# A two-layer encoder on one core: the last MLP's second product by Strassen's scheme, in chunks interleaved with the first product

## The chip, the cores and the metric

One Trainium2 chip, of which the kernel uses one core. The metric is the device time in microseconds of one execution of the whole program; the time before is the median of three runs.

## The reference

An encoder of two layers on 512 tokens of width 1024, in float32. Layer 0 mixes tokens by a retention and a sliding-window attention, layer 1 by an axial attention; each layer ends with an MLP of width 4096 with a squared ReLU. What matters here is the second line of the MLP:

```python
D_MODEL = 1024; SEQ = 512; DEPTH = 2; D_FF = 4 * D_MODEL

for layer in range(DEPTH):
    h = rms_norm(x, norm_mix[layer])
    ...
    x = x + y
    h = rms_norm(x, norm_mlp[layer])
    x = x + jnp.square(jax.nn.relu(h @ w_mlp_up[layer])) @ w_mlp_down[layer]
return x
```

Per layer `w_mlp_up` is 1024x4096 and `w_mlp_down` 4096x1024.

## The kernel before, in words

**Products.** TensorE multiplies in a rounded float32 form (fp32r). To keep float32's accuracy every operand is split into a high part, its rounded copy, and a low part, the rest; a product of two operands is three matmuls into one bank, high x high, high x low, low x high (`mm3`, L309). The high parts are written by casts on ScalarE, the low parts by subtractions on VectorE. A bank is a PSUM tile of 128x512; there are eight.

**Weights.** `w_stream` (L383) brings the weights in units of 256 rows by 512 columns, 512 KB: SyncE's queue loads a unit into one of two `raw` tiles, ScalarE casts it (`wh`, L406), VectorE subtracts (`wl`, L408). There are four pairs of `wh` and `wl` (the w pairs), given in turn to the units in the order of a list, `plan`; this cast and subtraction are called the unit's cut below. `gemm` (L413) makes a 512x512 result in four banks, in steps of 512 along the contracted dimension, two units a step.

**The MLP.** `mlp` (L1157) goes over D_FF in two halves. In each half four up products (h times W_up, 96 matmuls each) make 2048 rows of the hidden layer. Their results leave the banks by a ReLU and scaling on VectorE (L1168), a square on ScalarE (L1171) and a split into one of four `big` pairs (L299, L304). Then two down products of 192 matmuls (512 columns of the result each) run over the 2048. In the last MLP `last` (L1320) adds each bank to the accumulator `acc_o` (L1325), and in the second half stores the result (L1329). The very last 128 rows of the last down product are made in two halves of 256 columns (`halves=True`): 96 of that MLP's matmuls have 256 columns.

**What sets the order.** The kernel's parts are generators, run at build time by `Weave` (L120), a planner: each step says which engine it needs and for how long, by the costs of `vec`, `act` and `pe` (L189 to L198), and the planner always writes the instruction that can start first on its own clock. What it wrote is each engine's fixed order on the chip. Casts and subtractions of W carry a bias that lets other work go ahead unless the unit is among the next to be used. Products of the attention stages are woven in the same way with gemms that make the projections.

Of the kernel before, what the change touches and what calls it, by code (L numbers as in the profile page):

```python
# [12 lines left out]
F32 = mybir.dt.float32  # L13
F32R = mybir.dt.float32r
AF = mybir.ActivationFunctionType
# [48 lines left out]
class Slots:  # L64


    def __init__(self, weave, items):
        self.weave, self.waiting = weave, []
        self.free = [(0.0, i) for i in range(len(items))]
        self.items = items  # L70
        self.index = {id(x): i for i, x in enumerate(items)}

    def ask(self, task):
        if not self.free:
# [111 lines left out]
            self.advance(task, op[0])  # L186


def vec(n, scalars=0, rate=0.96):  # L189
    return ("V", 0.065 + n / rate / 1000 + 0.065 * scalars)  # L190


def act(n, extras=0):
    return ("A", 0.075 + n / 1200 + 0.093 * extras)


def pe(n):
    return ("P", 3 * (n / 2400 + 0.0025))  # L198


TRANSPOSE = 0.11
# [13 lines left out]
def hybrid_encoder(ctx: ExitStack, tc: tile.TileContext, a, out):  # L215
# [13 lines left out]
    psp = ctx.enter_context(tc.tile_pool(name="psp", bufs=1, space=PS))  # L229

    W = Weave()

    def slots(name, n, shape, dt, pool=cst):
# [11 lines left out]
    probs_t = pairs("pt", 3, (P, 512))  # L245
    temps = slots("t", 11, (P, 512), F32)
    gates = slots("g", 4, (P, 512), F32)
    hs = [(cst.tile([P, 512], F32R, name=f"hh{k}"), cst.tile([P, 512], F32R, name=f"hl{k}")) for k in range(KD)]
    xT = [cst.tile([P, 512], F32, name=f"xT{k}") for k in range(KD)]
    rB = cst.tile([P, 512], F32, name="rB")  # L250

    def kv_pair():
# [56 lines left out]
    def mm3(o, l, r, first, last):  # L309
        (lh, ll), (rh, rl) = l, r  # L310
        nc.tensor.matmul(o, lhsT=lh, rhs=rh, start=first, stop=False)  # L311
        nc.tensor.matmul(o, lhsT=lh, rhs=rl, start=False, stop=False)  # L312
        nc.tensor.matmul(o, lhsT=ll, rhs=rh, start=False, stop=last)  # L313

    def transposed(bank, parts):
        for j, p_ in enumerate(parts):
# [61 lines left out]
    w_used = [0]  # L378
    def landed(ev):
        yield Sleep(W.now + LANDING)  # L380
        ev.set()

    def w_stream():  # L383

        arrived = [W.event() for _ in plan]
        raw_of = [None] * len(plan)

        def loads():
            yield opened
            for i in range(2, len(plan)):  # L390
                raw_of[i] = yield raws
                yield Sleep(W.now + 1.2)
                yield ("D", 1.5)
                nc.sync.dma_start(out=raw_of[i], in_=plan[i][1].rearrange("(k p) n -> p k n", p=P))
                W.spawn(landed(arrived[i]), LOAD)
                if i == 3:
                    w_begun.set()

        W.spawn(loads(), LOAD)
        for i in range(2, len(plan)):  # L400
            pair = yield wparts
            yield arrived[i]
            hi, lo = pair
            hold = lambda: LOAD_BIAS if i >= w_used[0] + 2 else -1.0
            yield act(1024) + (hold,)
            nc.scalar.copy(out=hi, in_=raw_of[i])  # L406
            yield vec(1024) + (hold,)
            nc.vector.tensor_tensor(out=lo, in0=raw_of[i], in1=hi.bitcast(F32), op=ALU.subtract)  # L408
            raws.give(raw_of[i])
            w_tiles[i] = pair  # L410
            w_ready[i].set()

    def gemm(name, r0, r1, c0, lhs, natural, evac, cls=EVAC, bk=None, halves=False):  # L413

# [739 lines left out]
        bigs.give(y)  # L1154


    def mlp(l, h_ev, rB_ev, last, after=None):  # L1157
        for hf in range(2):
            u, u_ready = [], []
# [177 lines left out]
    def products():  # L1337
# [66 lines left out]
        W.spawn(natural_xs(hn_ready), AUX)  # L1404
# [62 lines left out]
```

## Time and profile before

| | |
|---|---|
| median of three runs | 1261.37 us (1261.25 to 1261.75) |
| the profiled execution | 1261.47 us, its span 1259.7 us |
| TensorE matmuls (PE) | 1254.3 us busy, 5880 instructions |
| TensorE weight loads (PEld, beside matmuls) | 1043.9 us busy |
| VectorE (DVE) | 698.7 us busy, 55% |
| ScalarE (ACT) | 526.8 us busy, 42% |
| GpSimd (POOL) | 1.6 us busy |
| granted TensorE clock | 1.00 on the mean |

The span is what the profiler saw of the kernel, from the first to the last instruction; the device time of the same execution is 1.8 us longer. Matmuls are pipelined: one of 512 columns is listed with some 0.39 us, while the next starts 0.23 us behind it, so what one costs is read from the distance of two starts. In the rows further down, "PE" are matmuls, "PEld" weight loads, and L-numbers are lines of the kernel. The number ahead of an operation in the timeline is its start from the begin of the span, the next its length; brackets tell what it waited for, where the profile shows one.

### The profile page before, as it was taken

What the parts mean: (1) busy time and instruction counts of PE and PEld (TensorE: products, weight loads), DVE (VectorE), ACT (ScalarE), POOL (GpSimd) and SP (SyncE); (2) the same over time, 40 slices, a digit from 0 to 9 for tenths busy, and PEclk for the clock granted to TensorE, in tenths of its full rate; (3) what the DMA queues carried; (4) which work ended last, traced back from release to release, by engine and by line L of the source; (5) the groups of instructions that cost most, each with busy time, mean ns of one, the idle gap of its engine ahead of it and who ended that gap; (6) DMA issues with size and microseconds to landing.
All of it is one profiled execution on the core that took longest, in us unless ns stands there. A gap on an engine that the chain in (4) does not pass through costs nothing.

```text
span 1259.7 us, 15049 instructions
## 1 busy us (share of the span) xinstructions
PE 1254.3 (100%) x5880; PEld 1043.9 (83%) x5880; DVE 698.7 (55%) x1248; ACT 526.8 (42%) x1015; POOL 1.6 (0%) x10
## 2 busy tenths in 40 slices
PE   9999999999999999999999999999999999999998
PEld 7888888888888888888888888888888888888887
DVE  6698668767676452324444268897745422444331
ACT  6676424344344342224333245776544311244210
POOL 0000000000000000000000000000000000000000
PEclk9999999999999999999999999999999999999999
DMA  6521322222143333233333233111323233333331
GB/s 187 182 87 35 101 84 84 67 84 84 50 126 96 90 96 101 89 98 100 101 100 101 85 89 95 34 34 34 101 84 85 100 100 100 100 100 99 101 120 51
DMA packets 63896, 115.13 MB, mean 91 GB/s; under 512 B 5245, under 2 KB 11431, under 8 KB 63568
## 3 DMA queue, kind: packets, MB, share of 16 engines
q1 hardware_dynamic: 63824, 114.16, 29.3%
q8 instruction: 46, 0.75, 0.2%
q14 instruction: 26, 0.21, 0.1%
HBM read 112.03 MB, written 4.21 MB: 92 GB/s over the span
## 4 chain that ended last, share of the span: by engine, by line
PE 99%; DMA 0%; ACT 0%; SPq 0%; issue 0%; DVE 0%
PE bank L311 31%; PE bank L313 31%; PE bank L312 31%; PE bank L317 4%; PE bank L534 1%; DMA x_nat<-in_x_dram 0%; SPq L493 0%; PE bank L1114 0%; ACT pth L299 0%; PE bank L654 0%; PE bank L1141 0%; ACT t L1271 0%; DVE acc_o L1325 0%; PE bank L605 0%
## 5 line engine op out<-in xcount | busy, mean ns | idle before, releaser
L408 DVE TENSOR_TENSOR wl<-raw,wh 128x1024 fp32r<-128x1024 f32 x198 | 240.7, 1219 | 302.0 <-ACT wh L406 299.6
L406 ACT CAST wh<-raw 128x1024 fp32r<-128x1024 f32 x198 | 207.6, 1051 | 385.0 <-PE bank L312 228.1
L311 PE MATMUL bank<-hh,wh 128*128 128x512 f32 x512 | 200.7, 392 | 0.0
L313 PE MATMUL bank<-hh,wl 128*128 128x512 f32 x512 | 199.3, 389 | 0.0
L312 PE MATMUL bank<-hl,wh 128*128 128x512 f32 x512 | 199.2, 389 | 0.0
L311 PE MATMUL bank<-bigh,wh 128*128 128x512 f32 x448 | 176.0, 393 | 0.0
L313 PE MATMUL bank<-bigh,wl 128*128 128x512 f32 x448 | 174.6, 390 | 0.0
L312 PE MATMUL bank<-bigl,wh 128*128 128x512 f32 x448 | 174.4, 389 | 0.0
L311 PE MATMUL bank<-wh,hh 128*128 128x512 f32 x368 | 146.5, 398 | 0.0
L313 PE MATMUL bank<-wh,hl 128*128 128x512 f32 x368 | 143.8, 391 | 0.0
L312 PE MATMUL bank<-wl,hh 128*128 128x512 f32 x368 | 143.5, 390 | 0.0
L311 PEld LDWEIGHTS bank<-hh,wh 128*128 128x128 f32 x512 | 96.1, 188 | 20.1 <-issue 0.5
L313 PEld LDWEIGHTS bank<-hh,wl 128*128 128x128 f32 x512 | 96.1, 188 | 20.1
L312 PEld LDWEIGHTS bank<-hl,wh 128*128 128x128 f32 x512 | 96.1, 188 | 20.0 <-issue 0.5
L312 PE MATMUL bank<-wl,bigh 128*128 128x512 f32 (+1 forms) x272 | 102.5, 377 | 0.0
L311 PE MATMUL bank<-wh,bigh 128*128 128x512 f32 (+1 forms) x272 | 102.4, 377 | 0.0
L313 PE MATMUL bank<-wh,bigl 128*128 128x512 f32 (+1 forms) x272 | 102.4, 377 | 0.0
L313 PEld LDWEIGHTS bank<-bigh,wl 128*128 128x128 f32 x448 | 84.1, 188 | 17.7
L311 PEld LDWEIGHTS bank<-bigh,wh 128*128 128x128 f32 x448 | 84.1, 188 | 17.0 <-DVE ptl L304 0.3
L312 PEld LDWEIGHTS bank<-bigl,wh 128*128 128x128 f32 x448 | 84.2, 188 | 16.9
L313 PEld LDWEIGHTS bank<-wh,hl 128*128 128x128 f32 x368 | 69.1, 188 | 14.8
L311 PEld LDWEIGHTS bank<-wh,hh 128*128 128x128 f32 x368 | 69.1, 188 | 14.3 <-issue 0.9
(175 smaller groups left out, 1569.9 us busy)
## 6 DMA issues: line engine op xcount, KB each, us to landing
raw<-in_w_mlp_up_dram SPq DMA_DIRECT2D x64, 512.0 KB, 3.7
raw<-in_w_mlp_down_dram SPq DMA_DIRECT2D x64, 512.0 KB, 4.4
raw<-in_w_in_even_dram SPq DMA_DIRECT2D x35, 512.0 KB, 4.0
raw<-in_w_out_even_dram SPq DMA_DIRECT2D x16, 512.0 KB, 3.6
raw<-in_w_in_odd_dram SPq DMA_DIRECT2D x12, 512.0 KB, 3.7
raw<-in_w_out_odd_dram SPq DMA_DIRECT2D x8, 512.0 KB, 3.5
bdr<-bdr SPq DMA_DIRECT2D x2, 1024.0 KB, 6.1
out_dram<-acc_o SPq DMA_DIRECT2D x7, 256.0 KB, 2.0
```

Source lines behind the costliest of these rows:

```text
L311: nc.tensor.matmul(o, lhsT=lh, rhs=rh, start=first, stop=False)
L312: nc.tensor.matmul(o, lhsT=lh, rhs=rl, start=False, stop=False)
L313: nc.tensor.matmul(o, lhsT=ll, rhs=rh, start=False, stop=last)
L317: nc.tensor.transpose(bank[:, j * P:(j + 1) * P], p_, ident)
L406: nc.scalar.copy(out=hi, in_=raw_of[i])
L408: nc.vector.tensor_tensor(out=lo, in0=raw_of[i], in1=hi.bitcast(F32), op=ALU.subtract)
L534: nc.tensor.matmul(first_bk[b], lhsT=hs[k][i == 2][:, b * P:(b + 1) * P], rhs=wt, start=k == 0 and i == 0, stop=False)
```

## The change

The second product of the last MLP is done by Strassen's scheme in Winograd's form: 2x2 blocks, seven products in place of eight, with sums of blocks ahead and behind. D_FF is taken in four chunks of 1024. In a chunk, the left operand's blocks are halves of the tokens (256) and of the chunk (512); the right operand's are halves of the chunk and of the columns (512). A product is 24 matmuls of 512 columns: two W units (h = 0, 1), for each two blocks of 128 tokens, two of 128 rows, three matmuls. Partial sums of the results stay in the banks: product 6 goes on in the banks of product 1 after these have been read, 7 in those of 6, 3 in those of 5.

- **Order of the products.** up(0), then for each chunk q: up(2q+1), products 2, 1, 4, then up(2q+2) if q < 3, then products 6, 5, 7, 3. The last chunk has no up product between products 4 and 6.
- **Sums of the hidden layer** (A, B, C, D): 64 operations of 128x256 on VectorE (`minus`, line 1325 of the changed kernel), and the splits that follow them.
- **Sums of W.** Two of the four block sums, used by products 7 and 5, are made by negating a loaded unit in place on ScalarE and adding another from DRAM with an accumulating DMA (`added`) of 512 KB, issued from GpSimd's queue: 16 of them. The other two, used by products 6 and 4, are made by VectorE (16 operations of 128x1024). So W_down is cut into 56 units in place of 32.
- **Adds of the results**: 64 of 128x512 (`add`, line 1398), in place of 15 of 128x512 and 2 of 128x256.
- **Room.** `g` and the probabilities of the attention get tiles of a size that the last MLP can use as five more raw tiles; the tiles of x^T serve as raw tiles and for a sum, too.
- **The planner.** `pe(512)` goes from 0.6475 to 0.6805 us for three matmuls in the whole program; the fixed part of `vec` and `act` goes to 0.15 and 0.19 us in the last MLP alone. Since the price of a matmul is new everywhere, the planner's order changes in all stages.

```diff
+FIXED = [0.065, 0.075]
+
+
 def vec(n, scalars=0, rate=0.96):
-    return ("V", 0.065 + n / rate / 1000 + 0.065 * scalars)
+    return ("V", FIXED[0] + n / rate / 1000 + 0.065 * scalars)
 
 
 def act(n, extras=0):
-    return ("A", 0.075 + n / 1200 + 0.093 * extras)
+    return ("A", FIXED[1] + n / 1200 + 0.093 * extras)
 
 
 def pe(n):
-    return ("P", 3 * (n / 2400 + 0.0025))
+    return ("P", 3 * (n / 2400 + 0.0135))
...
+    def shared(i, dt):
+        return cst.tile([P, 2, 512], dt, tag=f"sh{i}", name=f"sh{i}")
+
+    gs = [shared(i, F32) for i in range(2)]
+    pts = [shared(i, F32R) for i in range(2, 5)]
+    probs_t = Slots(W, [(t[:, 0, :], t[:, 1, :]) for t in pts])
...
+    gates = Slots(W, [t[:, j, :] for t in gs for j in range(2)])
...
-    plan += plan_mlp(1)
...
+    PRODUCTS = (2, 1, 4, 6, 5, 7, 3)
...
+    plan_up(0)
+    for q in range(4):
+        plan_up(2 * q + 1, [(q, r, c, h) for r, c in ((0, 1), (0, 0), (1, 0)) for h in range(2)])
+        plan_products(q, PRODUCTS[:3])
+        last_two = [(q, 1, 1, h) for h in range(2)]
+        if q < 3:
+            plan_up(2 * q + 2)
+        for at in last_two:
+            chunk_at[at] = len(loads_of)
+            loads_of.append(quarter(*at))
+        plan_products(q, PRODUCTS[3:])
...
+        def added(out, q, r, c, h):
+
+            yield ("D", 1.6)
+            nc.gpsimd.dma_start(out=out, in_=quarter(q, r, c, h).rearrange("(k p) n -> p k n", p=P), accum_op=ALU.add)
+            yield Sleep(W.now + 4.5)
...
+        def t1(q, h, st):
+
+            x = raw_of[chunk_at[q, 0, 0, h]]
+            yield st["cut", 1]
+            yield st["t2"]
+            yield act(1024) + due(q, 5, h, 6)
+            nc.scalar.mul(x, x, -1.0)
+            yield from added(x, q, 0, 1, h)
+            st["src", 5].set()
+
+        def sums(q, h, st):
+
+            r11, r12, r21, r22 = (chunk_at[q, r, c, h] for r in range(2) for c in range(2))
+            yield arrived[r12]
+            t3 = raw_of[r12]
+            yield act(1024)
+            nc.scalar.mul(t3, t3, -1.0)
+            yield from added(t3, q, 1, 1, h)
+            st["src", 7].set()
+            yield arrived[r11]
+            st["src", 1].set()
+            W.spawn(t1(q, h, st), LOAD)
+            t2 = st["x"] = yield xs
+            yield vec(1024) + due(q, 4, h, 6)
+            nc.vector.tensor_tensor(out=t2, in0=t3, in1=raw_of[r11], op=ALU.add)
+            st["src", 6].set()
+            st["t2"].set()
+            yield st["cut", 2]
+            t4 = raw_of[r21]
+            yield vec(1024) + due(q, 4, h, 4)
+            nc.vector.tensor_tensor(out=t4, in0=t4, in1=t2, op=ALU.subtract)
+            st["src", 4].set()
+            yield st["cut", 4]
+            raws.give(t4)
+            yield st["cut", 6]
+            xs.give(t2)
+            for pr, n in ((5, r11), (7, r12), (3, r22)):
+                yield st["cut", pr]
+                raws.give(raw_of[n])
...
+        def cut(i, pair, ready, get, done):
+            yield ready
+            hi, lo = pair
+            src = get()
+            hold = lambda: LOAD_BIAS if i >= w_used[0] + 2 else -1.0
+            yield act(1024) + (hold,)
+            nc.scalar.copy(out=hi, in_=src)
+            yield vec(1024) + (hold,)
+            nc.vector.tensor_tensor(out=lo, in0=src, in1=hi.bitcast(F32), op=ALU.subtract)
+            done()
+            w_tiles[i] = pair
+            w_ready[i].set()
...
+            def minus(out, x, y, op=ALU.subtract):
+                yield vec(256)
+                nc.vector.tensor_tensor(out=out, in0=x, in1=y, op=op)
...
+            def rest(i, t_, f):
+                c = yield temps
+                yield ev["A", i]
+                yield from minus(c[:, half[0]], t_[:, half[1]], f[:, half[1]], ALU.add)
+                yield from minus(c[:, half[1]], c[:, half[0]], t_[:, half[0]])
+                yield from split(*part("C", i, slice(0, 512)), c, 512)
+                ev["1", i].set()
+                W.spawn(rest2(i, t_, f, c), AUX)
+
+            def rest2(i, t_, f, c):
+                yield from minus(t_[:, half[0]], t_[:, half[0]], t_[:, half[1]])
+                yield from minus(f[:, half[0]], f[:, half[0]], c[:, half[1]])
+                temps.give(c)
+                yield from split(*part("A", i, half[1]), t_[:, half[0]], 256)
+                temps.give(t_)
+                ev["3", i].set()
+                yield from split(*part("D", i, half[0]), f[:, half[0]], 256)
+                ev["D", i].set()
+                temps.give(f)
...
+            of = {1: ("A", "A", 0, "X", True, ((0, 0),)), 2: ("B", "B", 0, "Y", True, ((0, 0),)),
+                  4: ("B", "B", 1, "V", True, ((1, 0),)), 6: ("C", "1", 1, "X", False, ((0, 1),)),
+                  5: ("C", "1", 0, "Z", True, ((1, 1),)), 7: ("A", "3", 1, "X", False, ((1, 0), (1, 1))),
+                  3: ("D", "D", 0, "Z", False, ((0, 1),))}
+            open_, read = {}, {}
...
+            def add(tb, bank, outs, closes, stores):
+                for rc_ in outs:
+                    t, c = 2 * rc_[0] + tb, rc_[1]
+                    o = acc_o[t, c]
+                    yield acc_ready[t, c]
+                    yield vec(512)
+                    nc.vector.tensor_tensor(out=o, in0=bank, in1=o, op=ALU.add)
+                    if closes and rc_ == outs[-1]:
+                        gbanks.give(bank)
+                    if stores:
+                        yield ("D", 0.8)
+                        nc.sync.dma_start(out=out[0, t * P:(t + 1) * P, c * 512:(c + 1) * 512], in_=o)
...
+            for pr in PRODUCTS:
+                name, evn, hf, bn, opens, rc_ = of[pr]
+                ws = []
+                for h in range(2):
+                    n = w_used[0] + h
+                    assert plan[n][0] == ("down1", q, pr, h), (plan[n][0], q, pr, h)
+                    yield w_ready[n]
+                    ws.append(w_tiles[n])
+                    for tb in range(2):
+                        if h == 0:
+                            if opens:
+                                open_[bn, tb] = yield gbanks
+                            else:
+                                yield read[bn, tb]
+                        for ii in range(2):
+                            i = 2 * h + ii
+                            yield ev[evn, i]
+                            uh, ul = ub[name]
+                            us = slice(hf * 256 + tb * P, hf * 256 + (tb + 1) * P)
+                            yield pe(512)
+                            mm3(open_[bn, tb], (uh[:, i, us], ul[:, i, us]), (ws[h][0][:, ii, :], ws[h][1][:, ii, :]),
+                                opens and i == 0, i == NT - 1, skip_group_check=not opens)
+                        if h == 1:
+                            read[bn, tb] = W.spawn(add(tb, open_[bn, tb], rc_, pr in (2, 4, 7, 3), q == 3 and pr in (1, 3, 7)), EVAC)
+                    wparts.give(ws[h])
+                w_used[0] += 2
+                for n in {7: "A", 5: "C", 3: "D", 4: "B"}.get(pr, ""):
+                    bigs.give(ub[n])
+                if pr == 4 and q < 3:
+                    yield from up(2 * q + 2, lambda i, bank, st=state[q + 1]: up1(i, bank, st))
...
-        yield from mlp(1, hn_ready, rB1, last)
+        yield from last_mlp(hn_ready, rB1)
```

**The last chunk on VectorE.** First the end of VectorE's order before: cuts of W, and the adds of the last down product.

```order
L408 TENSOR_TENSOR wl_80<-raw_77,wh_79 128x1024
L408 TENSOR_TENSOR wl_82<-raw_78,wh_81 128x1024
L408 TENSOR_TENSOR wl_84<-raw_77,wh_83 128x1024
L408 TENSOR_TENSOR wl_86<-raw_78,wh_85 128x1024
L1325 TENSOR_TENSOR acc_o<-bank_74,acc_o 128x512
L1325 TENSOR_TENSOR acc_o<-bank_69,acc_o 128x512
L1325 TENSOR_TENSOR acc_o<-bank_70,acc_o 128x512
L1325 TENSOR_TENSOR acc_o<-bank_71,acc_o 128x256
L1325 TENSOR_TENSOR acc_o<-bank_72,acc_o 128x256
```

Then VectorE's order in the changed kernel, from the second cut of product 5 (wl_86) on, in the last chunk: wl_80 is the low half of product 7's first unit, whose pair product 6's first unit held; bigl_90 is the low half of C, bigl_92 and bigl_94 are those of A and D; line 538 is the subtraction of a cut, 319 that of a split.

```order
L538 TENSOR_TENSOR wl_86<-xs_6823,wh_85 128x1024
L1325 TENSOR_TENSOR t_102<-t_102 128x256
L1325 TENSOR_TENSOR t_103<-t_103 128x256
L1325 TENSOR_TENSOR t_107<-t_107,t_109 128x256
L538 TENSOR_TENSOR wl_80<-sh_6526,wh_79 128x1024
L1325 TENSOR_TENSOR t_109<-t_110,t_105 128x256
L319 TENSOR_TENSOR bigl_92<-t_102,bigh_91 128x256
L1325 TENSOR_TENSOR t_109<-t_109,t_110 128x256
L1325 TENSOR_TENSOR t_106<-t_106,t_101 128x256
L319 TENSOR_TENSOR bigl_94<-t_107,bigh_93 128x256
L1325 TENSOR_TENSOR t_100<-t_100 128x256
L319 TENSOR_TENSOR bigl_90<-t_109,bigh_89 128x512
```

Where VectorE had cuts and adds alone, the cut of a later product now stands ahead of the sums and the split of the last quarter of C.

**The first axial group on TensorE.** ident transposes a block of q into a bank, which is then cast and subtracted into bigh_87 and bigl_88; kv and bigh_87 make the scores of a head; wh and hh are a projection. Before:

```order
L317 MATMUL bank_72<-ident,t_104 128x128 x4
L311 MATMUL bank_70<-wh_81,hh_120 128x512
L312 MATMUL bank_70<-wl_82,hh_120 128x512
L313 MATMUL bank_70<-wh_81,hl_121 128x512
L311 MATMUL bank_70<-wh_81,hh_122 128x512
L312 MATMUL bank_70<-wl_82,hh_122 128x512
L313 MATMUL bank_70<-wh_81,hl_123 128x512
L311 MATMUL bank_69<-kv,bigh_87 128x512
L312 MATMUL bank_69<-kv,bigh_87 128x512
L313 MATMUL bank_69<-kv,bigl_88 128x512
L311 MATMUL bank_72<-kv,bigh_87 128x512
```

The same place in the changed kernel:

```order
L332 MATMUL bank_75<-ident,t_100 128x128 x4
L326 MATMUL bank_69<-kv,bigh_87 128x512
L327 MATMUL bank_69<-kv,bigh_87 128x512
L328 MATMUL bank_69<-kv,bigl_88 128x512
L326 MATMUL bank_75<-kv,bigh_87 128x512
```

The bank of the transposes is used for scores nine matmuls later before, and three matmuls later now.

## Rows read from the trace of the kernel before

**Rows 1.** The page, part 1: busy time, share of the span, instructions.

```profile
PE 1254.3 (100%) x5880; PEld 1043.9 (83%) x5880; DVE 698.7 (55%) x1248; ACT 526.8 (42%) x1015; POOL 1.6 (0%) x10
```

**Rows 2.** The page, part 4: the chain that ended last, by engine.

```profile
PE 99%; DMA 0%; ACT 0%; SPq 0%; issue 0%; DVE 0%
```

**Rows 3.** Table of stretches (us): length, busy time and instructions by engine.

```profile
core 0: us, PE busy (x) PEld busy (x) DVE busy (x) ACT busy (x) POOL busy (x), PEclk, DMA share, GB/s
925.00:1200.00 275.00, 275.00 (x1215) 227.72 (x1214) 107.02 (x120) 89.75 (x112) 0.00 (x0) 1.00 0.31 96
760.00:880.00 120.00, 119.92 (x605) 98.58 (x604) 103.30 (x264) 83.36 (x220) 0.00 (x0) 1.00 0.14 45
60.00:150.00 90.00, 90.00 (x477) 77.16 (x476) 75.47 (x249) 59.07 (x173) 0.00 (x0) 1.00 0.25 74
1256.00:1258.00 2.00, 0.51 (x5) 0.31 (x3) 0.42 (x1) 0.00 (x0) 0.00 (x0) 1.00 0.26 91
1258.00:1259.70 1.70, 0.00 (x0) 0.00 (x0) 0.00 (x0) 0.00 (x0) 0.00 (x0) 0.85 0.16 52
...
770.00:790.00 20.00, 20.00 (x96) 15.99 (x95) 19.32 (x65) 15.23 (x55) 0.00 (x0) 1.00 0.22 73
```

**Rows 4.** Waits of TensorE's weight loads, 30 to 1250 us: total, times, longest.

```profile
PEld bank L311 <- ACT t L1271: 1.1, 3, 0.5
PEld bank L311 <- DVE ptl L304: 0.5, 2, 0.3
```

**Rows 5.** Timeline of TensorE, around the first matmul of 256 columns.

```profile
1241.51 0.39 PE L313 MATMUL bank<-wh,bigl 128*128 128x512 f32 x1
1241.74 0.39 PE L311 MATMUL bank<-wh,bigh 128*128 128x512 f32 x1
...
1242.53 0.28 PE L312 MATMUL bank<-wl,bigh 128*128 128x256 f32 x1
1242.65 0.28 PE L313 MATMUL bank<-wh,bigl 128*128 128x256 f32 x1
```

**Rows 6.** Groups by line and shape: count, busy us, mean ns, idle before.

```profile
L304 DVE TENSOR_TENSOR bigl<-t,bigh 128x512 fp32r<-128x512 f32 x64 | 44.3, 692 | 49.4 <-ACT bigh L299 49.4
...
L299 ACT CAST bigh<-t 128x512 fp32r<-128x512 f32 x64 | 39.8, 622 | 2.0
...
L1325 DVE TENSOR_TENSOR acc_o<-bank,acc_o 128x512 f32<-128x512 f32 x15 | 10.4, 692 | 35.3 <-PE bank L313 35.3
...
L1325 DVE TENSOR_TENSOR acc_o<-bank,acc_o 128x256 f32<-128x256 f32 x2 | 0.8, 424 | 1.8 <-PE bank L313 1.8
```

**Rows 7.** Timeline of ScalarE and VectorE in the last MLP: one W unit's cut.

```profile
938.75 1.05 ACT L406 CAST wh<-raw 128x1024 fp32r<-128x1024 f32 x1 [6.33 <-PE bank L312]
939.84 1.22 DVE L408 TENSOR_TENSOR wl<-raw,wh 128x1024 fp32r<-128x1024 f32 x1 [6.16 <-ACT wh L406]
```

**Rows 8.** DMA issues: count, KB of each, median us from issue to landing.

```profile
raw<-in_w_mlp_down_dram SPq DMA_DIRECT2D x64, 512.0 KB, 4.4
...
bdr<-bdr SPq DMA_DIRECT2D x2, 1024.0 KB, 6.1
out_dram<-acc_o SPq DMA_DIRECT2D x7, 256.0 KB, 2.0
x_nat<-in_x_dram SPq DMA_DIRECT2D x3, 512.0 KB, 8.7
...
out_dram<-acc_o SPq DMA_DIRECT2D x2, 128.0 KB, 1.7
```

**Rows 9.** Timeline in the first axial group: transposes, cast, subtract, scores.

```profile
781.81 0.60 PE L317 MATMUL bank<-ident,t 128*128 128x128 f32 x4
...
782.45 0.58 ACT L299 CAST bigh<-bank 128x512 fp32r<-128x512 f32 x1 [0.66 <-PE bank L317]
...
783.07 0.69 DVE L304 TENSOR_TENSOR bigl<-bank,bigh 128x512 fp32r<-128x512 f32 x1
...
784.34 0.39 PE L311 MATMUL bank<-kv,bigh 128*128 128x512 f32 x1
```

**Rows 10.** Timeline at the end: the last matmul and the last add.

```profile
1256.23 0.28 PE L313 MATMUL bank<-wh,bigl 128*128 128x256 f32 x1
1256.55 0.42 DVE L1325 TENSOR_TENSOR acc_o<-bank,acc_o 128x256 f32<-128x256 f32 x1 [1.01 <-PE bank L313]
```

More of the change, by code (lines that the diff above doesn't have):

```diff
@@ L71, in __init__, with add @@
         self.index = {id(x): i for i, x in enumerate(items)}
+    def add(self, item):
+        self.index[id(item)] = len(self.items)
+        self.items.append(item)
+        self.give(item)
     def ask(self, task):
@@ L307, in split, with mm3 @@
                                            op0=ALU.mult, op1=ALU.subtract)
-    def mm3(o, l, r, first, last):
+    def mm3(o, l, r, first, last, **kw):
         (lh, ll), (rh, rl) = l, r
-        nc.tensor.matmul(o, lhsT=lh, rhs=rh, start=first, stop=False)
-        nc.tensor.matmul(o, lhsT=lh, rhs=rl, start=False, stop=False)
-        nc.tensor.matmul(o, lhsT=ll, rhs=rh, start=False, stop=last)
+        nc.tensor.matmul(o, lhsT=lh, rhs=rh, start=first, stop=False, **kw)
+        nc.tensor.matmul(o, lhsT=lh, rhs=rl, start=False, stop=False, **kw)
+        nc.tensor.matmul(o, lhsT=ll, rhs=rh, start=False, stop=last, **kw)
     def transposed(bank, parts):
@@ L373, in hybrid_encoder, with plan_w, quarter, plan_up @@
             plan += w_parts("w_out_odd", r0, r0 + 512, c0)
-    plan += plan_mlp(1)
+    PRODUCTS = (2, 1, 4, 6, 5, 7, 3)
+    chunk_at = {}
+    loads_of = [ap for _, ap in plan]
+    def plan_w(parts):
+        plan.extend(parts)
+        loads_of.extend(ap for _, ap in parts)
+    unit_load = list(range(len(plan)))
+    at_product = {}
+    def quarter(q, r, c, h):
+        r0 = q * 1024 + (1 - r) * 512 + h * 256
+        return a["down1"][r0:r0 + 256, c * 512:c * 512 + 512]
+    def plan_up(g, between=()):
+        between = list(between)
+        for part in w_parts("up1", 0, D, g * 512):
+            for at in between[:1]:
+                chunk_at[at] = len(loads_of)
+                loads_of.append(quarter(*at))
+            del between[:1]
+            unit_load.append(len(loads_of))
+            plan_w([part])
+        for at in between:
+            chunk_at[at] = len(loads_of)
+            loads_of.append(quarter(*at))
+    def plan_products(q, prs):
+        for pr in prs:
+            for h in range(2):
+                at_product[q, pr, h] = len(plan)
+                plan.append((("down1", q, pr, h), None))
+                unit_load.append(None)
+    plan_up(0)
[6 more added lines that the diff above has]
+        for at in last_two:
+            chunk_at[at] = len(loads_of)
+            loads_of.append(quarter(*at))
+        plan_products(q, PRODUCTS[3:])
     w_ready = [W.event() for _ in plan]
@@ L383, in w_stream @@
     def w_stream():
-        arrived = [W.event() for _ in plan]
-        raw_of = [None] * len(plan)
+        arrived = [W.event() for _ in loads_of]
+        raw_of = [None] * len(loads_of)
+        chunks = {}
         def loads():
             yield opened
-            for i in range(2, len(plan)):
+            for i in range(2, len(loads_of)):
                 raw_of[i] = yield raws
@@ new lines, in plain, with source @@
+        def plain(q, pr, h, n):
+            yield arrived[n]
+            chunks[q, h]["src", pr].set()
+        def source(i):
+            if unit_load[i] is not None:
+                n = unit_load[i]
+                return arrived[n], lambda: raw_of[n], lambda: raws.give(raw_of[n])
+            _, q, pr, h = plan[i][0]
+            st = chunks[q, h]
+            qr = {1: (0, 0), 5: (0, 0), 2: (1, 0), 4: (1, 0), 3: (1, 1), 7: (0, 1)}.get(pr)
+            get = (lambda: st["x"]) if qr is None else (lambda: raw_of[chunk_at[(q,) + qr + (h,)]])
+            return st["src", pr], get, st["cut", pr].set
@@ L400, in w_stream @@
+        for q in range(4):
+            for h in range(2):
+                st = chunks[q, h] = {(k, p_): W.event() for k in ("src", "cut") for p_ in PRODUCTS}
+                st["t2"] = W.event()
+                W.spawn(sums(q, h, st), LOAD)
+                W.spawn(plain(q, 2, h, chunk_at[q, 1, 0, h]), LOAD)
+                W.spawn(plain(q, 3, h, chunk_at[q, 1, 1, h]), LOAD)
+        last = None
         for i in range(2, len(plan)):
             pair = yield wparts
-            yield arrived[i]
@@ L403, in w_stream @@
[L403 to L411, printed above, removed]
+            ready, get, done = source(i)
+            if last is not None and unit_load[i] is not None:
+                yield last
@@ L413, in gemm @@
+            last = W.spawn(cut(i, pair, ready, get, done), LOAD)
     def gemm(name, r0, r1, c0, lhs, natural, evac, cls=EVAC, bk=None, halves=False):
```

63 lines of the change are left out of this document (58 added, 5 removed).

## The prediction

> **What bounds the kernel now.** I read the page's busy line first: TensorE's matmuls are busy 1254.3 of 1259.7 us, VectorE 55%, ScalarE 42% [rows 1]. The chain that ended last is TensorE for 99% of the span [rows 2], so a matmul taken out is worth its whole slot, unless something that it covered becomes late. The table of stretches tells where that can happen [rows 3]: in the last MLP (925 to 1200 us) TensorE is full while VectorE is busy 107.0 of 275 us (39%); in the attention before it, 770 to 790 us, VectorE is busy 19.3 of 20 us, so there the matmuls barely cover VectorE. All that TensorE waits for outside the first 30 us is a few tenths at a time, the longest group being 1.1 us [rows 4].
>
> **What is removed.** One slot is the distance between two starts: 1241.51 to 1241.74, 0.227 us for 512 columns (1215 matmuls in 275.0 us give 0.2263), and 1242.53 to 1242.65, 0.12 us for 256 columns [rows 3, 5]. The last second product had 8 gemms of 96 slots = 768 slots' worth of 512 columns: 720 matmuls of 512 columns and 96 of 256. Strassen's form (Winograd's seven products) has 4 chunks x 7 products x 24 = 672 of 512. So 48 x 0.2267 = 10.9 us and 96 x 0.12 = 11.5 us go: **-22.4 us**, all on the path.
>
> **What is added, and its cover.** The up products stay at 768 matmuls, so the last MLP is 1440 x 0.2267 = 326 us of TensorE. VectorE must fit under it: 98 operations of 128x1024 (W's low halves and the two W sums) x 1.22, 128 of 128x512 x 0.69, 112 of 128x256 x 0.42 [rows 6, 7]: 120 + 88 + 47 = 255 us, 78%. ScalarE gets 24 casts more and 16 negations, each like the 1.05 us cast [rows 7]: 42 us, still under half. On the mean both fit, so I cost them at nothing, except where a chunk's own order leaves no cover.
>
> **The last chunk's stall.** In chunks 0 to 2 the next chunk's up product (96 matmuls, 21.8 us) stands between products 4 and 6, and everything product 6 needs is ready. The last chunk has none. There VectorE's order puts product 7's W cut (L538, wl_80) ahead of the low half of sum C's last split (bigl_90), which product 6's second half needs; product 7's cut needs the w pair that product 6's first half holds. So VectorE waits for TensorE, with C's last sums queued behind it, and then TensorE waits for VectorE. From the end of the first half: cast 1.05, handover 0.04, subtract 1.22 [rows 7], three 128x256 operations at 0.42 less their overlap, about 1.1, the cast of C 0.62 [rows 6], and some 0.4 of handovers: 4.4 us. TensorE has three matmuls that need none of it, 0.7 us. The low half (0.69) comes after three more 128x256 operations, about 0.5 us past TensorE's next cover. **+4.2 us**, between 3.5 (all overlaps good) and 5.
>
> **The tail.** The last add is 128x512 at 0.69 for 128x256 at 0.42 [rows 6], the last store 256 KB at 2.0 for 128 KB at 1.7 [rows 8]: **+0.6 us**.
>
> **The planner's new price.** pe() for 512 columns goes from 0.6475 to 0.6805 us for three matmuls (three slots measure 0.680), for the whole program. VectorE's price outside the last MLP stays 0.598 for an operation that takes 0.69 [rows 6]. So the planner now believes that TensorE covers 5% more of the others' work, and brings products nearer to what they wait for. One place shows it. In the first axial group of before the four transposes of q start at 781.81, the cast empties their bank at 782.45 to 783.03, the subtract at 783.07 to 783.76, and the score product into the same bank starts at 784.34, nine matmuls after the transposes: 0.6 us to spare [rows 9]. In the changed order three matmuls stand between: it would start six slots sooner, at 782.98, and must wait to 783.76 and a handover of some 0.2: about 1 us lost, on a VectorE that is full there [rows 3]. The rest of the attention is re-ordered too (VectorE 84% busy from 60 to 150 us, 86% from 760 to 880 [rows 3]); I can't price each place and take four such: **+4 us**, an estimate. Bounds: -3 (all waits of [rows 4] and its like gone) to +8 (twice as many).
>
> **The accumulating DMAs** (16, 512 KB each, GpSimd's queue). Nothing else stands in that queue, and GpSimd's engine is idle [rows 1]. No row shows one; the nearest are plain loads of the same size, 4.4 us, the DRAM copy of 1 MB, 6.1, and the slowest 512 KB loads, 8.7 [rows 8]. Room in the last chunk, counted from the end of its up product: product 1's two W units get the w pairs that the up product's last pass gives back (6 matmuls before its end, and at its end); with that product's squares and splits between them on both engines I put their cuts, the negations and the two DMAs at about 3.5 and 6. Product 5's cut can start when product 4's halves give their pairs back, at 60 x 0.2267 = 13.6 and 72 x 0.2267 = 16.3. So a landing within 10 us costs nothing, and each us beyond costs about one, once, because C's sums stand behind that cut on both engines. I take 0, by the row that moves the same bytes (4.4).
> The Trainium skill, "DMA: Bandwidth & Descriptors", section "Anatomy of one DMA — SWDGE (gpsimd) path", fits such a DMA as 2.0 us + bytes / 436e3; by it 512 KB is an estimated 3.2 us, and the sum would be the same. No run here shows that path yet.
>
> **Sum.** -22.4 + 4.2 + 0.6 + 4 = -13.6. The profiled execution took 1261.47, 1259.7 of it the span; it is 0.1 above the median of the three runs. 1261.47 - 13.6 - 0.1 = **1247.8, so 1248 us**.
>
> **Rivals.**
> *The re-plan costs nothing* (0 instead of +4): 1244; a gain of 3 besides: 1241. For it: before's waits are small [rows 4], and the new price agrees with the measured slot, so the planner sees TensorE more truly. Against: the place above, and VectorE still priced too low. Chance 0.2 for 1240 to 1244.
> *Late accumulating DMAs.* At 15 us from issue the last chunk loses 5 more: 1253; at 20, 1258. For it: an add reads its destination too, and VectorE is busy twice as much as before in that stretch. Against: the DMA engines' share is 0.31 there [rows 3]. Chance 0.13.
> The Trainium skill, "SBUF — State Buffer", section "Who interferes with whom", would give it a mechanism: descriptor generation for GpSimd's queue is starved while VectorE holds a port pair that the two share. The same section says that tensor_tensor has no such two-port mode; VectorE's rows in the last MLP here are TENSOR_TENSOR [rows 6, 7], so I leave the chance where it was.
> *Slower than before.* The same DMA at more than 26 us eats 16 us more, and the time passes 1264. It decides from there; no row of before has a 512 KB transfer of more than 8.7 us [rows 8]. Chance 0.05, and as much for a time between 1259 and 1264.
> *The seven products don't replace eight:* excluded, since the built program has 144 matmuls fewer (48 + 96).
> A fall of the clock belongs to the forecast's band: after the last matmul (1256.23) the granted clock is 1.00 until 1258 and 0.85 on the mean of the next 1.7 us [rows 3, 10], so TensorE, idle, began to lose the full level (2.4 GHz) for the half one (1.2 GHz) within that last stretch. A stall of 3.7 us may just reach that; half speed for as long again as the stall would cost 1.9 us.
>
> **Chances.** Forecast 0.57 (1244 to 1252), cheap re-plan 0.2 (1240 to 1244), late DMAs 0.13 (1252 to 1259), no visible change 0.05, slower 0.05. Leaving out the last two and the far end of the late DMAs, the range is 1241 to 1255. A measurement here tells some 0.2%, 2.5 us, from no change. Faster 0.90, same 0.05, slower 0.05.
>
> **What would show it.** Matmuls of 512 columns in the last MLP 0.227 apart, 144 fewer; one wait of TensorE of 3.5 to 4 us near the end for the ScalarE cast of bigh, followed by one of about 0.5 for VectorE; stores of 256 KB last. In the first axial group a wait of about 1 us for the score product into the transposes' bank, and waits in the attention that add to 4 us more than before. GpSimd's DMAs landing within 10 us. It is wrong if TensorE waits for W in chunks 0 to 2 (then VectorE's or ScalarE's order, not its sum, is late), if L538's cut of product 5 waits for a DMA, or if the attention's waits come to nothing or to over 8 us.

## The result, and the profile after

The changed kernel takes 1252.15 us (median; 1250.96 to 1252.68) beside 1261.42: ratio 0.9925, interval 0.9908 to 0.9942. The forecast was 1248 in 1241 to 1255. The profiled execution has a span of 1250.8 us, 8.9 less than before. (Of experiment 7's kernel a first run is left out, since its matmuls started 0.84 us apart in place of 0.23 and it took 4429.53 us, and one run of the kernel before beside it took 3273.61 us.)

The page of the changed kernel, parts 1 and 4:

```profile
PE 1235.5 (99%) x5736; PEld 1023.9 (82%) x5736; DVE 809.7 (65%) x1447; ACT 581.5 (46%) x1103; POOL 21.2 (2%) x26
...
PE 95%; DVE 3%; DMA 1%; issue 0%; ACT 0%; SPq 0%; DVEq 0%
```

Beside [rows 1, 2]: 144 matmuls fewer, 18.8 us less busy, and the chain is no longer TensorE's alone: 5% of it lies on others. What TensorE waited for, from 30 us to the end (total, times, longest):

```profile
PE bank L326 <- ACT bigh L314: 3.4, 1, 3.4
PE bank L326 <- ACT t L1550: 1.3, 1, 1.3
PE bank L332 <- ACT t L1550: 1.0, 1, 1.0
PE bank L326 <- DVE bigl L319: 0.6, 1, 0.6
PE bank L332 <- DVE t L999: 0.2, 1, 0.2
PE bank L328 <- DVE bigl L319: 0.2, 1, 0.2
```

Before there was no such line for matmuls at all past 30 us. The first and the last stand in the last chunk, the others in the attention. The table of stretches (columns as in [rows 3]):

```profile
760.00:880.00 120.00, 116.97 (x582) 95.40 (x581) 101.53 (x267) 82.04 (x218) 0.00 (x0) 0.99 0.11 36
...
916.00:1216.00 300.00, 300.00 (x1336) 248.23 (x1335) 216.24 (x305) 149.52 (x206) 17.05 (x14) 1.00 0.45 120
...
786.30:789.70 3.40, 3.34 (x8) 2.67 (x9) 3.21 (x16) 3.40 (x8) 0.00 (x0) 0.50 0.00 0
...
1221.80:1225.30 3.50, 0.14 (x1) 0.00 (x0) 3.02 (x8) 1.82 (x5) 0.00 (x0) 1.00 0.00 0
1226.60:1230.00 3.40, 3.40 (x9) 2.65 (x8) 2.20 (x5) 0.55 (x1) 0.00 (x0) 0.50 0.00 0
```

Three things are to be seen. In the last MLP, up to the last chunk, TensorE is full for 300 us with VectorE at 72%: the sums and splits are hidden there, as costed. From 1221.8 to 1225.3 TensorE does nothing. And twice the granted clock is at its half level (1.2 GHz) for 3.4 us, each time just behind waits.

**The account.** One matmul near the begin of the last MLP stands in the same place of the order in both kernels, with 4296 ahead of it; it divides the span:

```profile
909.71 0.79 PE L311 MATMUL bank<-hh,wh 128*128 128x512 f32 x1
```

```profile
915.91 0.79 PE L326 MATMUL bank<-hh,wh 128*128 128x512 f32 x1
```

The first is the kernel before, the second the changed one. I take the same matmul in every run below ("the mark"; in experiment 3, where the order beside it differs, the matmul with as many ahead), and the start of the last matmul. In experiments 1, 6, 7, 9 and 10 three matmuls stand ahead of the mark in place of four transposes, which puts it some 0.2 us later and the distance behind it as much shorter, with nothing lost. A mark is one profiled execution: experiment 8, which has the order of the kernel before, has it at 908.97, 0.7 us earlier.

| kernel | mark at | mark to last matmul | last matmul to end | span | median |
|---|---|---|---|---|---|
| before | 909.71 | 346.52 | 3.46 | 1259.7 | 1261.42 |
| changed | 915.91 | 329.80 | 5.06 | 1250.8 | 1252.15 |
| difference | +6.20 | -16.72 | +1.60 | -8.9 | -9.3 |

So what lies ahead of the last MLP, the attention above all, lost 6.2 us, the last MLP gained 16.7, and the end lost 1.6.

**The last chunk.** Timeline of the changed kernel (start, length, engine, line, operation, what it waited for):

```profile
1221.30 1.05 ACT L536 CAST wh<-sh 128x1024 fp32r<-128x1024 f32 x1 [1.66 <-PE bank L328]
...
1221.56 0.39 PE L328 MATMUL bank<-wh,bigl 128*128 128x512 f32 x1
...
1222.38 1.23 DVE L538 TENSOR_TENSOR wl<-sh,wh 128x1024 fp32r<-128x1024 f32 x1 [0.48 <-ACT wh L536]
1223.53 0.41 DVE L1325 TENSOR_TENSOR t<-t,t 128x256 f32<-128x256 f32 x1
...
1224.64 1.54 ACT L314 CAST bigh<-t 128x512 fp32r<-128x512 f32 x4 [1.68 <-DVE t L1325]
...
1225.32 0.50 PE L326 MATMUL bank<-wh,bigh 128*128 128x512 f32 x1 [3.37 <-ACT bigh L314]
...
1226.27 0.54 PE L328 MATMUL bank<-wh,bigl 128*128 128x512 f32 x1 [0.23 <-DVE bigl L319]
...
1227.04 0.63 PE L327 MATMUL bank<-wl,bigh 128*128 128x512 f32 x1
1227.46 0.63 PE L328 MATMUL bank<-wh,bigl 128*128 128x512 f32 x1
```

It is the chain of the prediction, link by link: the cast of product 7's unit starts when product 6's first half gives its pair back, the subtraction behind it takes 1.23, the last sum of C comes out of VectorE after that, the cast of C is waited for by TensorE. The start at 1225.32 is 3.76 us behind the one ahead of it, 3.5 more than a slot. The last two rows, 0.42 us apart, are the half clock.

**The first axial group**, where [rows 9] stand before:

```profile
782.96 0.60 PE L332 MATMUL bank<-ident,t 128*128 128x128 f32 x4
...
783.92 0.78 ACT L1550 ACTIVATE t<-bank,col,rqs 128x512 f32<-128x512 f32 x1 [1.91 <-DVE col L1548]
...
784.69 0.57 ACT L314 CAST bigh<-bank 128x512 fp32r<-128x512 f32 x1
...
784.84 0.50 PE L326 MATMUL bank<-kv,bigh 128*128 128x512 f32 x1 [1.28 <-ACT t L1550]
...
785.63 0.67 DVE L319 TENSOR_TENSOR bigl<-bank,bigh 128x512 fp32r<-128x512 f32 x1
...
786.36 0.79 PE L326 MATMUL bank<-kv,bigh 128*128 128x512 f32 x1 [0.55 <-DVE bigl L319]
```

The score product into the transposes' bank waits for the low half (0.55), as foreseen; the one ahead of it waits for the exponentials that free its own bank (1.28), which was not. Together they lose 2.2 us, and then the clock falls.

The 6.2 us can be followed from place to place, by the starts of matmuls that have as many of each shape ahead in both kernels. The changed kernel is 1.2 us behind at 777 us of its span, 3.4 when the second of these score products starts, and 5.0 when the clock is back. The rest comes at one more place, where transposes wait for the exponentials, 1.2 us more than a slot:

```profile
843.03 0.40 PE L328 MATMUL bank<-bigh,wl 128*128 128x512 f32 x1
844.47 0.66 PE L332 MATMUL bank<-ident,t 128*128 128x128 f32 x4 [1.04 <-ACT t L1550]
```

**The end and the DMAs.** The last matmul and the last add, and the two transfers in question:

```profile
1245.71 0.39 PE L328 MATMUL bank<-wh,bigl 128*128 128x512 f32 x1
1246.13 0.69 DVE L1398 TENSOR_TENSOR acc_o<-bank,acc_o 128x512 f32<-128x512 f32 x1 [0.67 <-PE bank L328]
```

```profile
sh<-in_w_mlp_down_dram POOLq DMA_DIRECT2D x11, 512.0 KB, 5.9
...
out_dram<-acc_o SPq DMA_DIRECT2D x8, 256.0 KB, 2.0
```

Over all 16 the accumulating DMAs land in 5.6 to 10.0 us, median 6.0.

### The profile page after: what moved, and what is told of

Read it like the earlier page. It is cut to its first block, busy times and chain, and to the rows that moved or that the text cites. A ratio compares the mean times of both kernels' runs of the same rounds, so it can differ in the third digit from the quotient of the medians.

```text
span 1250.8 us, 15112 instructions
## 1 busy us (share of the span) xinstructions
PE 1235.5 (99%) x5736; PEld 1023.9 (82%) x5736; DVE 809.7 (65%) x1447; ACT 581.5 (46%) x1103; POOL 21.2 (2%) x26
## 4 chain that ended last, share of the span: by engine, by line
PE 95%; DVE 3%; DMA 1%; issue 0%; ACT 0%; SPq 0%; DVEq 0%
PE bank L326 30%; PE bank L328 30%; PE bank L327 30%; PE bank L332 3%; PE bank L680 1%; DVE wl L538 1%; DVE col L1545 1%; DMA x_nat<-in_x_dram 1%; DVE bigl L319 0%; DVE t L974 0%; SPq L639 0%; DVE xT L1223 0%; PE bank L1260 0%; DVE t L999 0%; DVE bigl L321 0%
## 5 line engine op out<-in xcount | busy, mean ns | idle before, releaser
L538 DVE TENSOR_TENSOR wl<-raw,wh 128x1024 fp32r<-128x1024 f32 x153 | 186.1, 1219 | 170.0 <-ACT wh L536 168.2
L536 ACT CAST wh<-raw 128x1024 fp32r<-128x1024 f32 x153 | 160.4, 1051 | 244.9 <-PE bank L327 191.6
L326 PE MATMUL bank<-wh,bigh 128*128 128x512 f32 x224 | 88.0, 393 | 3.4 <-ACT bigh L314 3.4
L328 PE MATMUL bank<-wh,bigl 128*128 128x512 f32 x224 | 87.8, 392 | 0.2 <-DVE bigl L319 0.2
L327 PE MATMUL bank<-wl,bigh 128*128 128x512 f32 x224 | 87.8, 392 | 0.0
L319 DVE TENSOR_TENSOR bigl<-t,bigh 128x512 fp32r<-128x512 f32 (+1 forms) x112 | 61.8, 573 | 34.4 <-ACT bigh L314 34.4
```

The source lines that it names most:

```text
L319: nc.vector.tensor_tensor(out=lo, in0=src, in1=hi.bitcast(F32), op=ALU.subtract)
L328: nc.tensor.matmul(o, lhsT=ll, rhs=rh, start=False, stop=last, **kw)
L536: nc.scalar.copy(out=hi, in_=src)
L538: nc.vector.tensor_tensor(out=lo, in0=src, in1=hi.bitcast(F32), op=ALU.subtract)
```

## Experiments

Two theories of the 6.2 us stood against each other: the planner's new price, or the rest of the change (the new W stream, the shared tiles) that re-orders the attention, too. And two of the 3.5 us: the one cut that waits for TensorE, or a backlog on VectorE.

**1. The old price in the attention** (changed kernel; the third number of FIXED is set at the program's begin, and again at that of the last MLP).

```diff
 def pe(n):
-    return ("P", 3 * (n / 2400 + 0.0135))
+    return ("P", 3 * (n / 2400 + FIXED[2]))
...
-    FIXED[:] = 0.065, 0.075
+    FIXED[:] = 0.065, 0.075, 0.0025
...
-        FIXED[:] = 0.15, 0.19
+        FIXED[:] = 0.15, 0.19, 0.0135
```

> The changed kernel with the planner's old price of a matmul (0.6475 us for three of 512 columns) in all stages but the last MLP, which keeps 0.6805. Theory (the new price thins the covers of the attention): the last MLP begins some 6 us sooner, at 909.7 to 910.5 us of the span in place of 915.9, no fall of the clock near 786 us, and the time is 1246 us (1245 to 1247). Rival (the new W stream and the shared tiles re-order the attention, not the price): the last MLP still begins at 914 to 917 us and the time is 1250 to 1253.

Measured: 1246.64 us (1246.38 to 1247.24), ratio 0.988 (0.9865 to 0.9895); mark at 910.33, and what TensorE waited for past 30 us is the last chunk alone:

```profile
PE bank L326 <- ACT bigh L314: 3.4, 1, 3.4
PE bank L328 <- DVE bigl L319: 0.2, 1, 0.2
```

5.6 of the 6.2 us are back by one number of the planner. The W stream and the shared tiles alone cost 0.6; 0.2 of it is the order beside the mark, and the rest is less than two profiles of one order differ by.

**2. The new price alone** (kernel before).

```diff
-    return ("P", 3 * (n / 2400 + 0.0025))
+    return ("P", 3 * (n / 2400 + 0.0135))
```

> The kernel before with the new price of a matmul (0.6805 us for three) and nothing else. Theory (the price alone costs it): the last MLP begins at 915 to 917 us of the span in place of 909.7, TensorE waits for the exponentials of the first axial group, and the time is 1267.5 us (1266 to 1269). Rival (the W stream and the shared tiles cost it): 1261 to 1263.

Measured: 1264.36 us (1263.85 to 1265.14), ratio 1.0019 (1.0009 to 1.0028); mark at 912.22. The price alone costs 2.5 us at the mark (2.7 by the medians): neither expectation. The place is the same, and the waits are shorter:

```profile
783.92 0.50 PE L311 MATMUL bank<-kv,bigh 128*128 128x512 f32 x1 [0.76 <-ACT t L1271]
...
785.39 0.50 PE L311 MATMUL bank<-kv,bigh 128*128 128x512 f32 x1 [0.51 <-DVE bigl L304]
```

1.3 us of waits in place of 1.8, no fall of the clock, and no wait where the changed kernel has one at 844 us. So of 6.2: 2.5 by the price, 0.6 by the rest, and 3.1 that come only where both meet: 1.5 the clock (see 5), 1.2 the place at 844 us, 0.4 the longer waits of the first axial group. Why the two meet there is a matter of the planner's order, and no run takes it apart further.

**3. The price moved as far the other way** (kernel before).

```diff
-    return ("P", 3 * (n / 2400 + 0.0025))
+    return ("P", 3 * (n / 2400 - 0.0085))
```

> The kernel before with the price of a matmul moved as far the other way (0.6145 us for three of 512 columns). Theory (a low price makes the planner put more matmuls ahead of what waits, a high one fewer): no loss, 1259.5 to 1262 us, and the score product stands at least nine matmuls behind the transposes of its bank. Rival (before's order is a lucky one, and any other price costs some us): 1263.5 to 1268.

Measured: 1262.81 us (1261.57 to 1264.63), ratio 1.0007 (0.9998 to 1.0017). That can't be told from no change, and is 0.8 over the theory's own bound. Of the mark's 1.2 us more, 0.6 had come by the hundredth matmul, in the loads of the start. The score product stands six matmuls behind the transposes of its bank there, not nine. So a lower price loses little, but it doesn't put more matmuls ahead of what waits.

**4. Product 7's first cut in the last chunk held back** until C is split (changed kernel; `c_split` is set behind C's fourth split).

```diff
         def cut(i, pair, ready, get, done):
             yield ready
+            if plan[i][0][:2] == ("down1", 3) and plan[i][0][2:] in ((7, 0),):
+                yield c_split
```

> The changed kernel, with the cut of product 7's first W unit in the last chunk held back until all four quarters of C are split. Theory (VectorE and ScalarE wait for TensorE at that cut, with C's last sums behind it): the wait of 3.4 us ahead of product 6's second half falls to about 1.9 us, that for the low half grows to about 1, since the sums now stand only behind product 5's second cut; no fall of the clock near 1227; the time is 2.5 us less, 1249.6 (1248.5 to 1250.3). Rival (C's sums are late from VectorE's backlog, not from that cut): the time stays within 0.8 us of 1252.15.

Measured: 1250.26 us (1247.84 to 1251.74), ratio 0.9906 (0.9891 to 0.9921); mark to last matmul 327.12, 2.7 us less. The waits of the last chunk:

```profile
PE bank L326 <- ACT bigh L314: 2.3, 1, 2.3
PE bank L328 <- DVE bigl L319: 0.2, 1, 0.2
```

The wait is 1.1 us shorter (1.5 were expected), the one for the low half stays at 0.2 (it was expected to grow to about 1), and the clock stays up there, which is the other 1.6. The intervals of this run and of the changed kernel overlap; the verdict is the trace's.

**5. Product 5's second cut held back, too.**

```diff
-            if plan[i][0][:2] == ("down1", 3) and plan[i][0][2:] in ((7, 0),):
+            if plan[i][0][:2] == ("down1", 3) and plan[i][0][2:] in ((5, 1), (7, 0)):
```

> As the last, with the cut of product 5's second W unit held back, too. Theory: nothing that waits for TensorE past product 4's adds stands ahead of C's sums; the two waits are 0.5 to 0.7 us each, the clock stays at the full level, and the time is 4.3 us less than 1252.15, 1247.8 (1247 to 1249). Rival (backlog): no less than in the run with one cut held back; or product 5 or 7 waits for its W, and the gain is given back behind product 6.

Measured: 1248.05 us (1246.92 to 1249.21), ratio 0.9892 (0.9876 to 0.9909); mark to last matmul 325.82, 4.0 less than the changed kernel's 329.80. In the last chunk there is left

```profile
PE bank L328 <- DVE bigl L319: 0.8, 2, 0.6
```

and one start that comes 0.7 us late for it in product 7, a small part of what the rival said would be given back. This run tells another thing. In its first axial group TensorE waits as long as in the changed kernel (starts 1.55 and 0.95 us apart in both), but the clock does not fall:

```profile
786.30:789.70 3.40, 2.99 (x13) 2.47 (x14) 3.40 (x16) 3.40 (x11) 0.00 (x0) 1.00 0.00 0
```

13 matmuls in place of 8. For the 150 matmuls around that place (from the 3650th), which stand in the same order in both, the changed kernel takes 32.7 us and this run 31.2: 1.5 us are the clock's. The run of experiment 4 had the fall there. The same order of the same instructions can go either way, by 1.5 us, about the spread of the changed kernel's own runs (1.7).

**6. Both repairs.** The edits of 1 and 5 together.

> The changed kernel with both: the old price of a matmul ahead of the last MLP, and the cuts of product 5's second and product 7's first W unit in the last chunk held back until C is split. Theory (the two losses are separate places and add up): 5.5 and 4.1 us less than 1252.15, so 1242.6 us (1241.8 to 1243.6), no fall of the clock before the last matmul. Rival (they share something, so that one gain takes part of the other): 1244 to 1247.

Measured: 1244.4 us (1243.45 to 1245.97), ratio 0.986 (0.9844 to 0.9876). That beats both kernels, by 17 us and by 7.8, but not by the 9.6 that the two add up to, and it lies in the rival's range. By the trace they do add up: mark to last matmul 325.55 (329.55 in experiment 1), mark at 911.50, of which 1.0 us had come by the hundredth matmul, in the loads of the start, which the edits don't touch. I count the missing 1.9 us to the start's scatter, without having shown it for more than 1.0 of it in the profiled run.

**7. Plain loads in place of the accumulating DMAs** (on 6; the second addend of two of W's block sums is left out).

```diff
-            nc.gpsimd.dma_start(out=out, in_=quarter(q, r, c, h).rearrange("(k p) n -> p k n", p=P), accum_op=ALU.add)
+            nc.gpsimd.dma_start(out=out, in_=quarter(q, r, c, h).rearrange("(k p) n -> p k n", p=P))
```

> The run with both repairs and plain loads in place of the 16 accumulating DMAs once more (the second addend of two of W's block sums is left out), for its time. Theory (nothing waits for these DMAs): 1243.4 to 1246, the range of the kernel with the accumulating DMAs; landing 4.0 to 4.6 us. Rival (an accumulating DMA holds something up): under 1242.4.

Measured: 1243.0 us in two runs (1242.85 and 1243.14), between the two expectations; but mark to last matmul is 325.56 us, as with accumulating (325.55), so TensorE loses nothing to these DMAs in the last MLP. The 0.6 us between the two profiled runs had come by the hundredth matmul (24.67 and 25.25 us). Two of SyncE's own loads, issued at 963 and 1045 us beside these DMAs, land in 9.2 and 7.2 us with the adding and in 4.5 and 4.9 without; that doesn't reach TensorE either. Landing, of this kernel and then of 6:

```profile
sh<-in_w_mlp_down_dram POOLq DMA_DIRECT2D x11, 512.0 KB, 4.5
```

```profile
sh<-in_w_mlp_down_dram POOLq DMA_DIRECT2D x11, 512.0 KB, 5.8
```

So the adding costs 1.3 us of the landing, and GpSimd's queue next to nothing against the 4.1 to 4.5 of plain loads on SyncE's.

**8. Sixteen tiny DMAs on GpSimd's queue** (kernel before; nobody reads them).

```diff
+    pad = cst.tile([P, 16], F32, name="pad")
...
         W.run()
+        for i in range(16):
+            nc.gpsimd.dma_start(out=pad[:, i:i + 1], in_=a["down1"][0:P, i:i + 1])
```

> The kernel before with 16 tiny DMAs added on GpSimd's queue early in the program, which nobody reads. Theory (the program's end waits for each of that queue's semaphores in turn, which is half of what the change's end lost): the distance from the last matmul's start to the end of the span grows from 3.46 us to 4.0 to 4.4, and before that nothing moves. Rival (the longer end is the larger store and add alone): it stays at 3.4 to 3.6 us.

Measured, in one run: last matmul to end 3.74 us for 3.46, less than expected; and experiment 3, without such DMAs, has 3.76. In the trace SyncE's sequencer waits, once the last store has landed, for further semaphores one after another, some 0.07 us each: about 0.25 us before, 0.45 here, 0.9 in the changed kernel. The theory is right in kind and explains a part. The semaphore steps of each of these four traces have one pause of some 0.35 us: before and here it falls while the store is still on its way and costs nothing, in experiment 3 and in the changed kernel it falls behind the landing. So of the changed kernel's 0.9 us from the landing to the end (1.93 for 1.02), four more steps are 0.27, the pause is 0.36, and what follows takes 0.3 longer (1.05 for 0.75).

**9. Measured prices for VectorE and ScalarE, too** (changed kernel). If the new price of a matmul costs because VectorE's stays too low beside it, honest prices for all should mend it.

```diff
-    FIXED[:] = 0.065, 0.075
+    FIXED[:] = 0.15, 0.19
```

> The changed kernel with the new price of a matmul everywhere, and the fixed parts of VectorE's and ScalarE's prices at 0.15 and 0.19 us in the whole program, as in the last MLP (512 elements: 0.683 and 0.617, against 0.69 and 0.59 to 0.63 measured). Theory (the new price of a matmul costs because VectorE's stays too low beside it): the last MLP begins at 909.5 to 912 us of the span and the time is 1247 us (1246 to 1249). Rival (the price of a matmul itself, or any new order): it begins at 914 us or later and the time is 1250 or more.

Measured: 1259.53 us (1258.58 to 1261.43), ratio 0.9978 (0.9969 to 0.9987); mark at 921.73, 12 us later than before. The theory falls; the rival (914 us or later) holds, and the loss is larger than it asked for. What TensorE waited for, first lines:

```profile
PE bank L326 <- ACT bigh L314: 4.0, 2, 3.4
PE bank L327 <- DVE sh L319: 2.5, 4, 0.9
PE bank L332 <- DVE t L946: 1.4, 2, 1.0
PE bank L332 <- DVE sh L319: 1.1, 1, 1.1
```

The first line has the last chunk's 3.4 in it; the others are waits in places that had none, most of them for the splits of the probabilities (sh).

**10. The same with the two cuts held back.**

> As the last, with the two cuts of the last chunk held back until C is split. Theory: 4 us less than the last one's time by the profile's last MLP (325.5 us from its first matmul to its last, in place of some 329.5); 1243 us (1242 to 1245). Rival (C's sums are late for another reason in this order): the last MLP stays over 328 us.

Measured: 1253.96 us (1253.51 to 1255.06), ratio 0.9939 (0.9926 to 0.9953); mark to last matmul 325.59, in place of 330.37 in 9. The time missed, since the mark comes at 921.34, but the repair of the last chunk is worth as much in a third order: 4.0 us (5), 4.0 (6), and 4.8 here, where the clock had been low for 6.8 us in place of 3.4.

## Why the prediction was right, point by point

- **What bounds the kernel** held: TensorE's slots, and beside them single places where a cover is too thin. VectorE at 72% (78% was the estimate) cost nothing on the mean.
- **What is removed**, -22.4: without the waits left in experiment 5 (0.3, 0.4 and 0.7 us past a slot) the last MLP would take 324.4 us from the mark, 22.1 less than before's 346.52. Right.
- **The last chunk's stall**, +4.2: 3.5 and 0.4 of waits are 3.9, at the place, for the reason and by the chain named; experiments 5, 6 and 10 take it away by moving that cut and product 5's (0.7 us past a slot are left there). They leave VectorE the same work in another order, so a backlog was not the cause. That one cut is a third of it: with it alone moved (4), 2.3 us of wait stay, since product 5's second cut waits for TensorE as well, which the prediction did not price by itself.
- **The fall of the clock**, left out of the sum: it came behind that stall, 1.2 GHz for 3.41 us, some 1.6 us. In the sum the last chunk was 5.4, not 4.2. A second one in the attention was not thought of.
- **The planner's new price**, +4: this is the term that was mis-sized, 6.2 at the mark. The bounds -3 to +8 held it. The place named lost 2.2 us in place of 1, and 1.5 more by the clock; the place at 844 us was not named, and 1.2 had been lost before the first axial group. The 4 was one place priced and three more taken unseen, so that 6.2 came that near to it is partly luck. The reason was wrong in part: the price by itself costs 2.5; it takes the new W stream beside it to make 6.2. And the argument that the planner now believes in too much cover is not borne out: a lower price doesn't gain (3), and honest prices lose 12 us (9). What the runs support is plainer: at the mark the old costs with the new stream are 0.6 us later than before's own, the lower price 1.2, the new price 2.5, and 6.2 with the new stream, measured prices 12. None gains, and only the last three stand clear of the 0.7 us by which two profiles of one order differ, and of the start's scatter (0.6 of the 1.2).
- **The accumulating DMAs**, 0: right; they land in 5.6 to 10.0 us, and the last MLP is as long without the adding (7).
The Trainium skill, "DMA: Bandwidth & Descriptors", section "Anatomy of one DMA — SWDGE (gpsimd) path", gave by its fit an estimate of 3.2 us for such a transfer. The trace has 4.5 for plain loads on that queue and 5.9 for accumulating ones, both from the begin of GpSimd's issuing instruction, which takes 1.2 us itself; the measurement decides, and neither changes the sum.
The Trainium skill, "SBUF — State Buffer", section "Who interferes with whom", lets tensor_tensor out of the instructions that starve that queue; the trace agrees as far as it goes: with VectorE busy 72%, some nine tenths of it by TENSOR_TENSOR, plain loads on that queue land in 4.5 us, as on SyncE's (4.1 to 4.5). No run here has the other kind beside these DMAs.
- **The tail**, +0.6: it is 1.6. The last add is 0.27 longer, as said; the last store takes about 0.3 us more to land, as said; the close of the program behind it takes 0.9 us longer, which the prediction left out (taken apart in experiment 8), and 0.1 lies between the last matmul and the last add.
- **The sum**: -22.1 + 5.4 + 6.2 + 1.6 = -8.9 for -13.6. Each loss came out larger than its term (the last chunk's by the fall of the clock), the attention's by most. By its number 1252.15 lies just past the band of the forecast (1244 to 1252), in that of the late DMAs, whose mechanism did not come: all 16 landed within the 10 us that the prediction allowed. The range had its upper end, 1255, from that rival; the upper bounds of the forecast's own terms (5, 0.6 and 8) add up to 1252.6. So the range was met partly by luck, while the mechanism was the forecast's. None of the three signs of being wrong came: TensorE waited for no W, product 5's cuts in the last chunk waited for TensorE and for no DMA, and the attention lost neither nothing nor over 8 us.

## What to carry to other kernels

Price a saving on the bottleneck engine by its slots, then walk the ends of the pipeline (the last chunk, the tail) by each engine's order: what was free in the middle has no cover there, and an in-order engine that waits for a late buffer holds up all that stands behind it. Where a planner writes the order from a table of costs, treat a change of one cost as a change of every stage, and measure it apart from the algorithm: a more truthful cost gave the worse order here. With the two repaired (old cost ahead of the last MLP, two cuts behind the sums) the same algorithm takes 1244.4 us in place of 1252.15.

## What the runs showed of the hardware

- TensorE's granted clock fell to 1.2 GHz for 3.41 us behind a wait of 3.4 us (the changed kernel and experiment 1; for 6.8 us in experiment 9), but also behind two waits of 1.3 and 0.55 us with three matmuls between, in two profiles of three with the same order there (the changed kernel and experiment 4, not 5). Either fall of 3.41 us took some 1.5 us. Behind a wait of 2.3 us (experiment 4, last chunk) the clock stayed at 2.4 GHz.
- An accumulating DMA of 512 KB lands in 5.8 to 5.9 us where a plain one on the same queue takes 4.5. The queue's packets are nearly twice as many for the same bytes (of experiment 6 and of 7):

```profile
q0 software_dynamic: 4352, 8.39, 4.1%
```

```profile
q0 software_dynamic: 2304, 8.39, 2.1%
```
